# Twice the room for the software DMA queue's descriptors, and two DRAM writes placed later in the loop

## The chip, the cores and the metric

The kernel runs on one core of one Trainium2 chip. The metric is the device time of one execution in microseconds. The kernel before takes 748.84 us (median of 3 runs, 746.74 to 749.02).

A core has a matrix engine (TensorE, PE; its weight loads are shown as PEld), VectorE (DVE), ScalarE (ACT), GpSimd (POOL) and a queue for transfers (SyncE, SP). Each engine works through its own list of instructions in order; semaphores tie the lists together. All times of single instructions are from one profiled execution and count from the start of its span.

## What is computed

One layer of a hybrid encoder on 512 frames of width 1024, in float32. Cut to what matters here:

```python
hn   = rms_norm(x, norm1_g)
proj = hn @ w_in                         # q, k, v of two attentions, and two gates
out_a = chunked_attention(qa, ka, va, ...)        # 8 heads x 64, softmax
out_b = stick_breaking_attention(qb, kb, vb)      # 8 heads x 64
mixed = sigmoid(gate_a) * (out_a @ w_branch_a) + sigmoid(gate_b) * (out_b @ w_branch_b)
x = x + mixed @ w_out
hid = rms_norm(x, norm2_g) @ w_ffn_up    # 1024 -> 2 x 2816
hid = causal_depthwise_conv_width_3(hid) + conv_b
gate, up = hid[:, :2816], hid[:, 2816:]
x = x + (silu(gate) * up) @ w_ffn_down   # 2816 -> 1024
```

The change touches the last four lines: the way from the up-projection to the down-projection.

## The kernel before, in words

**Precision.** A float32 product is made of three matmuls in a reduced format: each operand is split into a high part (a cast, on ACT) and a low part (the operand minus the high part, on DVE), and high x high, high x low and low x high are summed. So every weight block that SP loads (`raw`) is split into `whi` (ACT, L271 or L242) and `wlo` (DVE, L276 or L243) before PE can use it. A split of block j+1 is issued while PE works on block j.

**The up-projection** is a loop over 22 blocks of 128 gate columns and 128 up columns (`up0` to `up21`, L1229). Ten blocks are plain products of 128x512 (L300 to L302). Twelve (`SEVEN`) are done with seven products in place of eight, in 128x256 pieces (L1171); their sums of weights were made earlier, put into DRAM (`parked`) and are loaded again by `fetch_extra` (L230) into `wxh`, `wxl`, `w2h`, `w2l`. After a block's products come bias and convolution (`conv`, L990 to L993), SiLU (L1014) and the product of gate and up (L1089) into one of four places of `ub`.

**Pairs.** After every second block, `pair_sums(i)` turns two places of `ub` into the operands of the down-projection. Three sums and one difference are made on DVE (`sums`, L1044), some into `st`, a buffer of which there is one. The results are then split into high and low parts in two tiles: `ax` (the first combination, 2048 wide) and `ay` (the second, 1536 wide). For pair 0 and for pairs 9 and 10, ACT casts and DVE subtracts (`halves`). For pairs 1 to 8, `by_dma` (L1056) does the subtraction in the transfer: ACT writes the negative of the high part into the low part's place (L1061), a transfer on POOL's queue adds the source to it (L1062, `accum_op=ALU.add`), and ACT casts the high part (L1063). That makes four accumulating transfers a pair: in the program's order on POOL `ay<-ub` (128x256), `ax<-st` (128x256), `ax<-ub` (128x768) and `ay<-st` (128x512). The next pair's first sum writes `st`, so it has to wait until `ay<-st` of this pair has landed.

**Kept in DRAM.** `ay` of pairs 0 to 6 is written to `ayd` by POOL right after the pair (L1095); it is read back by `fetch` (L1126) on the same queue. `ax` of pairs 0 and 1 is written to `axd` by SP (L1097) and read back by SP at L1236, after `up18` and after `up21`.

**Order.** The program is written in one order, and a scheduler then sets each engine's list from it (with priorities in a few places). [...]

The lines that the prediction speaks of: L133 to L148 (loads of weight blocks), L230 (parked sums), L161 and L1269 (split and products of the down-projection), L1044, L1061 to L1063, L1089, L1095, L1097, L1126 and L1191.

Of the kernel before, what the change touches and what calls it, by code (L numbers as in the profile page):

```python
# [8 lines left out]
F32 = mybir.dt.float32  # L9
# [6 lines left out]
P = 128  # L16
# [58 lines left out]
def block_kernel(ctx: ExitStack, tc: tile.TileContext, x, xt, params, g2, rbx, wts, wd0, wd1, out):  # L75
    nc = tc.nc
    V, A, G, PE, SP = nc.vector, nc.scalar, nc.gpsimd, nc.tensor, nc.sync
# [4 lines left out]
    sm = ctx.enter_context(tc.tile_pool(name="sm", bufs=1))  # L82
# [5 lines left out]
    def apool(name):  # L88
        return ap_ctx.enter_context(tc.tile_pool(name=name, bufs=1))
# [2 lines left out]
        apool(n) for n in ("pv", "pst", "pqn", "ppt", "pwk", "po")]  # L92
    pool_c = apool("pc")
    pool_pk = apool("ppk")
    par = sm.tile([P, 280], F32, tag="par", name="par")
    A.dma_start(par[:, 0:8], params[:, 0:8])
    A.preload_act_table_set("exp_and_others")
    WARM = 9
# [190 lines left out]
    def run_chunk(key, body, pieces=4):  # L289

        sp = split_gen(pos[key] + 1, pieces)
        for _ in body(*splits.pop(key)):
            next(sp, None)
            yield
        for _ in sp:
            pass
# [17 lines left out]
    axd = dram.tile([2, P, 2048], F32, tag="axd", name="axd")  # L314
# [668 lines left out]
    pairs = {}  # L983
# [4 lines left out]
    def conv(ps, tile_idx, c):  # L988
        cw = lambda j: par[:, C_CW + 2 * NF * j + tile_idx:C_CW + 2 * NF * j + tile_idx + 1]
        tap = A.activation(c, ps, AF.Identity, scale=cw(2), bias=par[:, C_CB + tile_idx:C_CB + tile_idx + 1])  # L990
        late["tap"] = (tap,)
        V.scalar_tensor_tensor(c[:, 1:], ps[:, 0:S - 1], cw(1), c[:, 1:], op0=ALU.mult, op1=ALU.add)
        V.scalar_tensor_tensor(c[:, 2:], ps[:, 0:S - 2], cw(0), c[:, 2:], op0=ALU.mult, op1=ALU.add)  # L993
# [17 lines left out]
    def gate(j, pg):  # L1011
        g = fp.tile([P, S], F32, tag="cg", name=f"cg{j}", bufs=1)
        conv(pg, j, g)
        A.activation(g, g, AF.Silu)  # L1014
        return g
# [68 lines left out]
    def up_fin(j, pg, pu, g=None):  # L1084
        if g is None:
            g = gate(j, pg)
        u = ub[:, j % 4, :]
        conv(pu, NF + j, u)
        late["fin"] = (V.tensor_tensor(u, g, u, op=ALU.mult),)  # L1089
        if j % 2 == 1 and j // 2 < 9:  # L1090
            steps = pair_sums(j // 2)
            for step in steps:
                step()
            if j // 2 < 7:
                G.dma_start(ayd[j // 2], pairs[j // 2][1].bitcast(F32))  # L1095
            if j // 2 < 2:
                SP.dma_start(axd[j // 2], pairs[j // 2][0].bitcast(F32))  # L1097

    def up_body(j):
        def body(hi, lo):  # L1100
            pg, pu = BANK(f"pg{j}", j - 1), BANK(f"pu{j}", j - 1)
            yield from up_mm(pg, hi, lo, 0, 0, S)
            g = gate(j, pg)
            if j in (2, 3):
                next(late["ts"])
            held = [] if j + 1 in SEVEN else None
            yield from up_mm(pu, hi, lo, P, 0, S, held)

            def end():
                for mm in held or ():  # L1110
                    mm()
                up_fin(j, pg, pu, g)
            if held:
                late["end"] = end
            else:
                end()
            if j in (2, 3):
                next(late["ts"])
        return body

    def fetch(i):

        tag = {0: "wxh", 1: "wxl", 6: "ax"}.get(i, "ts")
        n, bufs = {"wxh": (1600, 1), "wxl": (1600, 1), "ts": (2048, 4), "ax": (2048, 6)}[tag]
        ay = fp.tile([P, n], F32R, tag=tag, name=f"ay{i}", bufs=bufs)[:, 0:1536]
        G.dma_start(ay, ayd[i])  # L1126
        pairs[i] = (pairs[i][0], ay)
# [31 lines left out]
    def up_seven(j):  # L1159
        def body(hi, lo, wh, wl):  # L1160
# [40 lines left out]
            V.tensor_tensor(hu[:, left], b7, hu[:, right], op=ALU.add)  # L1201
            V.tensor_tensor(hu[:, right], hu[:, right], pc[:, 1], op=ALU.add)
            up_fin(j, None, hu, g)
            yield
        return body
# [4 lines left out]
    def up_first(j):  # L1210
        def body(hi, lo):
            pg, pu = BANK(f"pg{j}", 0), BANK(f"pu{j}", 0)
            halves.append((hi, lo, pg, pu))
            yield from up_mm(pg, hi, lo, 0, 0, 256)
            yield from up_mm(pu, hi, lo, P, 0, 256)
            if j == 1:
                n = 0
                for i, (h, l, g, u) in enumerate(halves):
                    for o, ps in ((0, g), (P, u)):
                        for _ in up_mm(ps, h, l, o, 256, S):  # L1220
                            n += 1
                            if n == 1 or 4 <= n < 8:
                                next(late["ts"])
                            yield
                    up_fin(i, g, u)
        return body

    late["ts"] = token_sums()
    for j in range(NF):  # L1229
        body = up_first(j) if j < 2 else up_seven(j) if j in SEVEN else up_body(j)  # L1230
        for _ in run_chunk(f"up{j}", body, pieces=4 if j < 2 else 2):
            pass
        if j in (SECOND[-1] + 1, SEVEN[-1] + 1):
            i = int(j == SEVEN[-1] + 1)
            ax = fp.tile([P, 2048], F32R, tag=("w2l", "ts")[i], name=f"ax{i}b", bufs=(1, 4)[i])
            SP.dma_start(ax.bitcast(F32), axd[i])  # L1236
            pairs[i] = (ax, pairs[i][1])
            for k in range(5 * i):
                fetch(k)
# [196 lines left out]
```

## Time and profile before

| what | value |
|---|---|
| median of 3 runs | 748.84 us (746.74 to 749.02) |
| the profiled execution | 752.24 us |
| its span, first to last instruction | 750.5 us |
| mean granted clock of PE | 0.986 |
| busy: PE, DVE, ACT, POOL | 720.6, 587.7, 432.7, 86.0 us |
| transfers of the software queue | 7264 packets, 20.45 MB |
| transfers of SP's and ACT's queues (hardware) | 133.81 MB |

How to read it: the engines work beside each other, so a busy time is no share of the sum. An engine's idle time is of use only where it is the engine that sets the end, and here PE is busy for 96% of the span. The profile tells for an idle stretch what ended it ("<-"); where a wait is for several things, it is put down to the one that came last by its records. "issue" means that nothing that the profile shows was waited for. The table of stretches gives each engine's busy microseconds between two times.

### The profile page before, as it was taken

The page shows a single profiled execution, that of the slowest core. Times are in us where ns is not written, and L with a number is a line of the kernel's source. Part 1 is how long each engine was busy: PE and PEld are TensorE (multiplying, and loading weights), DVE is VectorE, ACT ScalarE, POOL GpSimd, SP SyncE. Part 2 cuts the span into 40 slices and gives each one's busy share as a digit, 9 for nine tenths or more (in the row PEclk, how much of TensorE's full clock was granted, in tenths as well). Part 3 has the DMA queues.
Part 4 walks back from the last instruction along what each step waited for, and adds up shares of the span by engine and source line. Part 5 has one row for each costly group of instructions (what it writes and reads, how often), then busy time and mean ns, then how long its engine had stood idle before and what let it go on. Part 6 is the DMA issues. An engine that isn't in the chain of part 4 may idle for free.

```text
span 750.5 us, 11266 instructions
## 1 busy us (share of the span) xinstructions
PE 720.6 (96%) x4091; PEld 630.7 (84%) x4091; DVE 587.7 (78%) x1049; ACT 432.7 (58%) x803; POOL 86.0 (11%) x123
## 2 busy tenths in 40 slices
PE   9999999999999999999999998986998979999997
PEld 7889998888988888888898898885988869788886
DVE  6678779778999998694667985475848849899687
ACT  7486567577767675342365675455747745544541
POOL 2501300001111121000030011111111121000000
PEclk9999999999999999999999999998998989999999
DMA  9713336352563655769579589875766859765463
GB/s 320 273 58 97 100 106 216 127 196 113 169 221 143 190 203 206 253 228 339 222 280 295 211 261 310 241 219 160 232 169 183 253 141 339 269 211 196 169 224 112
DMA packets 51863, 154.97 MB, mean 206 GB/s; under 512 B 5600, under 2 KB 12384, under 8 KB 44000
## 3 DMA queue, kind: packets, MB, share of 16 engines
q1 hardware_dynamic: 44256, 133.67, 50.7%
q0 software_dynamic: 7264, 20.45, 10.6%
q8 instruction: 32, 0.52, 0.3%
q14 instruction: 23, 0.19, 0.1%
q10 hardware_dynamic: 288, 0.14, 0.1%
HBM read 116.49 MB, written 30.41 MB: 196 GB/s over the span
## 4 chain that ended last, share of the span: by engine, by line
PE 79%; DMA 6%; issue 6%; ACT 4%; DVE 4%; POOL 0%; DVEq 0%; SPq 0%; ACTq 0%; POOLq 0%
PE P L1269 13%; PE p L1171 8%; DMA ay<-st 4%; PE vA L433 3%; PE uA L433 3%; PE gB L300 2%; PE qkB L302 2%; PE gB L301 2%; PE qkB L300 2%; PE gB L302 2%; PE qkB L301 2%; PE wo L300 2%; PE wo L302 2%; PE wo L301 2%; PE pg L300 2%
## 5 line engine op out<-in xcount | busy, mean ns | idle before, releaser
L165 ACT CAST whi_dn<-raw_dn 128x1024 fp32r<-128x1024 f32 x33 | 34.4, 1050 | 26.2 <-DMA raw_dn<-in_wd 13.5
L1269 PE MATMUL P<-whi_dn,ax 128*128 128x512 f32 x144 | 44.7, 390 | 0.0
L161 DVE TENSOR_TENSOR wlo_dn<-raw_dn,whi_dn 128x1024 fp32r<-128x1024 f32 x33 | 40.1, 1223 | 3.6 <-ACT whi_dn L165 3.6
L300 PE MATMUL pg<-hth,whi_up 128*128 128x512 f32 (+1 forms) x96 | 34.9, 364 | 7.2 <-ACT whi_up L271 7.2
L1269 PE MATMUL P<-whi_dn,ay 128*128 128x512 f32 x132 | 40.8, 389 | 0.0
L744 POOL TENSOR_SCALAR_AFFINE_SELECT bB<-bB 128x128 f32<-128x128 f32 x32 | 21.9, 688 | 143.9 <-DVE bB L743 135.2
L1171 PE MATMUL p<-ts,whi_up 128*128 128x256 f32 x192 | 37.0, 288 | 0.0
L1044 DVE TENSOR_TENSOR st<-ub 128x256 f32<-128x256 f32 x11 | 4.6, 421 | 40.1 <-DMA ay<-st 31.5
L1171 PE MATMUL p<-hth,whi_up 128*128 128x256 f32 x96 | 28.2, 294 | 8.0 <-ACT whi_up L242 8.0
L302 PE MATMUL pg<-hth,wlo_up 128*128 128x512 f32 (+1 forms) x96 | 34.7, 361 | 1.2 <-DVE wlo_up L276 1.2
L301 PE MATMUL pg<-htl,whi_up 128*128 128x512 f32 (+1 forms) x96 | 34.7, 362 | 0.0
L207 DVE TENSOR_TENSOR pkr<-pkr 128x512 f32<-128x512 f32 x40 | 27.4, 685 | 8.7 <-DMA pkr<-in_wts 4.3
L300 PE MATMUL pu<-hth,whi_up 128*128 128x512 f32 (+1 forms) x90 | 31.8, 354 | 0.2 <-DVE hg L1197 0.2
L1269 PEld LDWEIGHTS P<-whi_dn,ax 128*128 128x128 f32 x144 | 27.0, 188 | 5.9 <-ACT whi_dn L165 0.3
L301 PE MATMUL pu<-htl,whi_up 128*128 128x512 f32 (+1 forms) x90 | 31.8, 353 | 0.0
L302 PE MATMUL pu<-hth,wlo_up 128*128 128x512 f32 (+1 forms) x90 | 31.5, 350 | 0.0
L1171 PEld LDWEIGHTS p<-ts,whi_up 128*128 128x128 f32 x192 | 31.2, 199 | 0.1
L1171 PE MATMUL p<-hth,wlo_up 128*128 128x256 f32 x96 | 28.1, 293 | 2.7 <-DVE wlo_up L243 2.7
L1171 PE MATMUL p<-ts,wlo_up 128*128 128x256 f32 x96 | 27.8, 289 | 2.6 <-DVE wlo_up L243 2.6
L243 DVE TENSOR_TENSOR wlo_up<-raw_up,whi_up 128x1024 fp32r<-128x1024 f32 x24 | 28.8, 1217 | 0.6 <-ACT whi_up L242 0.6
L1269 PEld LDWEIGHTS P<-whi_dn,ay 128*128 128x128 f32 x132 | 24.8, 188 | 5.1
L1269 PE MATMUL P<-wlo_dn,ax 128*128 128x512 f32 x72 | 28.1, 391 | 0.9 <-DVE wlo_dn L161 0.9
(350 smaller groups left out, 2566.9 us busy)
## 6 DMA issues: line engine op xcount, KB each, us to landing
parked<-pkr SPq DMA_DIRECT2D x45, 256.0 KB, 3.0
raw_dn<-in_wd SPq DMA_DIRECT2D x11, 1024.0 KB, 5.4
pkr<-in_wts SPq DMA_DIRECT2D x10, 1024.0 KB, 6.9
raw_up<-in_wts SPq DMA_DIRECT2D x10, 1024.0 KB, 6.6
raw_up<-in_wts SPq DMA_DIRECT2D x12, 512.0 KB, 6.1
raw_dn<-in_wd SPq DMA_DIRECT2D x11, 512.0 KB, 3.4
wxl_up<-parked SPq DMA_DIRECT2D x21, 256.0 KB, 5.9
ayd<-ay POOLq DMA_DIRECT2D x7, 768.0 KB, 3.9
```

Source lines behind the costliest of these rows:

```text
L161: chain("halves", V.tensor_tensor(o, x, y, op=op))
L165: chain("casts", A.copy(hi[:, sl], src))
L207: V.tensor_tensor(b[o], b[x], b[y], op=op)
L243: V.tensor_tensor(l[:, sl], src[:, sl], h[:, sl].bitcast(F32), op=ALU.subtract)
L300: ins = PE.matmul(ps, sh, mh, start=first, stop=False)
L301: PE.matmul(ps, sh, ml, start=False, stop=False)
L302: PE.matmul(ps, sl, mh, start=False, stop=last)
L433: PE.matmul(pss[t], st[:, 4 * half + k, t * P:(t + 1) * P], mv[:, k, :], start=half == 0 and k == 0 and j == 0, stop=half == 1 and k == 3 ...
L744: G.affine_select(b[:, n - P:n], b[:, n - P:n], pattern=[[-1, P]], compare_op=ALU.is_gt, fill=0.0, base=0, channel_multiplier=1)
L1044: return [V.tensor_tensor(o, x, y, op=op) for o, x, y, op in ((s1, u0[:, hi_], u1[:, hi_], ALU.add), (u0[:, hi_], u0[:, lo_], u0[:, hi_], ...
L1171: PE.matmul(ps, st, mv[:, k, :], start=first and k == 0 and n == 0, stop=last and k == 3 and n == 2, skip_group_check=True)
L1269: chain("products", PE.matmul(dst, st, mv, start=first and n == 0, stop=last and n == 2, skip_group_check=True))
```

## The change

Three edits. The region for the software queue's descriptors becomes 1024 bytes of a partition instead of 512. The tile `par`, of which 186 columns are used, is cut from 280 to 192 columns, 352 bytes a partition. The writes of `ax` to `axd` are no longer in `up_fin`, after pairs 0 and 1 (blocks 1 and 3); they are in the loop over blocks, after block 6 for pair 0 and after block 9 for pair 1.

```diff
-    par = sm.tile([P, 280], F32, tag="par", name="par")
+    par = sm.tile([P, 192], F32, tag="par", name="par")
...
             if j // 2 < 7:
                 G.dma_start(ayd[j // 2], pairs[j // 2][1].bitcast(F32))
-            if j // 2 < 2:
-                SP.dma_start(axd[j // 2], pairs[j // 2][0].bitcast(F32))
...
         for _ in run_chunk(f"up{j}", body, pieces=4 if j < 2 else 2):
             pass
+        if j in (6, 9):
+            SP.dma_start(axd[j // 9], pairs[j // 9][0].bitcast(F32))
...
-    nc = bacc.Bacc("TRN2", target_bir_lowering=False, num_devices=1, dynamic_dma_scratch_size=512)
+    nc = bacc.Bacc("TRN2", target_bir_lowering=False, num_devices=1, dynamic_dma_scratch_size=1024)
```

What the scheduler makes of it is seen in the engines' lists. First SP, at the second write to `axd` (pair 1), in the kernel before; `raw_up` is the load of a weight block in three parts, `wxl_up`, `w2h_up` and `w2l_up` are parked sums, and the numbers behind the names count the buffers as the program makes them:

```order
L230 DMA wxl_up_4767<-parked 128x512
L141 DMA raw_up_4762<-in_wts 128x512
L142 DMA raw_up_4762<-parked 128x512
L143 DMA raw_up_4762<-in_wts 128x1024
L1097 DMA axd<-ax_4593 128x2048
L230 DMA w2h_up_4904<-parked 128x512
L230 DMA w2l_up_4905<-parked 128x512
```

The same place on SP in the changed kernel:

```order
L230 DMA wxl_up_4765<-parked 128x512
L141 DMA raw_up_4760<-in_wts 128x512
L142 DMA raw_up_4760<-parked 128x512
L143 DMA raw_up_4760<-in_wts 128x1024
L1232 DMA axd<-ax_4592 128x2048
L230 DMA w2h_up_4902<-parked 128x512
L230 DMA w2l_up_4903<-parked 128x512
```

The write comes from another line of the code (L1232 instead of L1097) and stands between the same two loads; the first write to `axd`, 13 rows earlier, has kept its place as well. Only the buffers' numbers differ. POOL's list at pair 1 and the start of pair 2, in the kernel before:

```order
L1062 DMA ay_4594<-ub 128x256
L1062 DMA ax_4593<-st_4595 128x256
L1062 DMA ax_4593<-ub 128x768
L1062 DMA ay_4594<-st_4595 128x512
L1095 DMA ayd<-ay_4594 128x1536
L1062 DMA ay_4851<-ub 128x256
```

And in the changed kernel:

```order
L1062 DMA ay_4593<-ub 128x256
L1062 DMA ax_4592<-st_4594 128x256
L1062 DMA ax_4592<-ub 128x768
L1062 DMA ay_4593<-st_4594 128x512
L1095 DMA ayd<-ay_4593 128x1536
L1062 DMA ay_4849<-ub 128x256
```

Nothing has moved here either. The lists of all five engines are the same in both kernels, row by row, and so are the semaphores that each instruction waits for; addresses of tiles differ, and lines behind L1095 are counted two lower up to L1230 (L1126 is L1124 there).

## The prediction

> **What bounds the kernel now.** I read the busy times by stretch first, then who waited for whom, then the time lines of POOL, DVE and ACT around those waits. In the stretch view a row gives the stretch, its length, the busy us of PE, PEld, DVE, ACT and POOL with counts, the granted clock, the DMA share and GB/s.
>
> ```profile
> 438.00:618.00 180.00, 156.83 (x1044) 143.63 (x1044) 121.10 (x195) 108.24 (x188) 30.14 (x37) 0.95 0.74 213
> ```
>
> This is the up-projection with its pairs. PE is idle for 180.00 - 156.83 = 23.2 us of it, while DVE and ACT are far from full. PE is what the kernel is made of, so any gain must come out of these 23.2 us. Who ended PE's waits in the whole run, with total, count and longest:
>
> ```profile
> PE p L1171 <- ACT whi_up L242: 8.0, 2, 4.7
> PE pg L300 <- ACT whi_up L271: 7.2, 1, 7.2
> PE p L1171 <- DVE wlo_up L243: 5.3, 4, 2.1
> PE pg L302 <- DVE wlo_up L276: 1.2, 1, 1.2
> PE p L1171 <- DMA w2h_up<-parked: 1.2, 1, 1.2
> ...
> PE P L1269 <- DVE wlo_dn L161: 0.9, 1, 0.9
> ```
>
> The first five are the idle time of the stretch (22.9 of 23.2): PE wants the next weight block, and its high part (ACT) or low part (DVE) isn't made. A split is one cast and one subtraction a half, so they came late because something stood ahead of them in their queues:
>
> ```profile
> DVE st L1044 <- DMA ay<-st: 31.5, 5, 8.4
> ACT ax L1061 <- DVE st L1044: 30.7, 5, 8.4
> ```
>
> DVE stands at the first sum of a pair (L1044, into the only st buffer) until the last accumulating transfer of the pair before, the one that reads st, has landed; ACT stands behind DVE at L1061. The gaps also cost clock. More rows of the stretch view, the first three right after the three longest PE gaps, the last three without any gap:
>
> ```profile
> 512.25:519.08 6.83, 4.65 (x11) 3.69 (x12) 5.81 (x8) 6.83 (x11) 0.85 (x1) 0.50 0.51 145
> 566.87:573.70 6.83, 6.19 (x29) 6.19 (x30) 6.39 (x8) 6.83 (x10) 1.73 (x2) 0.50 0.47 119
> 614.65:621.48 6.83, 5.07 (x22) 4.78 (x23) 6.54 (x8) 6.83 (x10) 1.72 (x2) 0.50 0.65 139
> 391.00:459.00 68.00, 68.00 (x456) 62.24 (x455) 51.60 (x74) 40.20 (x63) 4.91 (x7) 1.00 0.77 249
> 520.00:564.00 44.00, 44.00 (x299) 40.70 (x297) 29.12 (x50) 23.56 (x42) 7.01 (x9) 1.00 0.70 197
> 619.00:651.00 32.00, 32.00 (x173) 27.57 (x171) 27.37 (x40) 15.74 (x24) 3.56 (x6) 0.96 0.94 333
> ```
>
> At half clock the matmuls of the first three rows took 4.65 + 6.19 + 5.07 = 15.9 us; at full clock they take 8.0 us less.
>
> Why the last transfer of a pair lands so late stands on POOL (start, duration, what it issues, idle time before it); below it the time to landing of the first three transfers, asked one at a time:
>
> ```profile
> 438.32 0.93 POOL L1062 DMA_DIRECT2D ay<-ub  x1 [4.87 <-ACT ay L1063]
> 444.18 0.86 POOL L1062 DMA_DIRECT2D ax<-st  x1 [4.92 <-ACT cg L1014]
> 448.02 0.87 POOL L1062 DMA_DIRECT2D ax<-ub  x1 [2.98 <-ACT cg L990]
> 452.28 0.85 POOL L1062 DMA_DIRECT2D ay<-st  x1 [3.39 <-issue]
> 459.96 0.56 POOL L1095 DMA_DIRECT2D ayd<-ay  x1 [6.83 <-DMA ay<-st]
> 460.57 0.87 POOL L1062 DMA_DIRECT2D ay<-ub  x1
> ```
>
> ```profile
> DMA to landing us min/median/max: 5.5/5.5/5.5
> DMA to landing us min/median/max: 3.5/3.5/3.5
> DMA to landing us min/median/max: 4.0/4.0/4.0
> ```
>
> 438.32 + 5.5 = 443.8, and the second goes out at 444.18; 444.18 + 3.5 = 447.7, the third at 448.02; 448.02 + 4.0 = 452.0, the fourth at 452.28. Each leaves 0.3 us after the one before it has landed; the releasers named in brackets are ACT instructions that don't make its input. So one accumulating transfer is in flight at a time. A plain one beside it is allowed: at 460.57 an accumulating one follows the plain write of ayd at once. Two accumulating ones don't fit, one and a plain one do. I read this as descriptor room: it is what the change doubles.
>
> **The change part by part.** *The write of axd.* The instructions of all five engines stand in the same places with the same waits before and after; the loop's later statement is scheduled where the old one was. Cost and gain: nothing by itself. What stands there still matters: SP waits at the second write, with six parked loads and a weight load queued behind it.
>
> ```profile
> SPq L1097 <- DMA ax<-ub: 10.3, 1, 10.3
> ```
>
> It waits for the third transfer above (issued 448.02, landed 452.0). That wait shrinks with the room; the 1.2 us in which PE waits for w2h is its price and goes with it.
>
> *The smaller par tile and the addresses.* No instruction more or less; what lies behind it moves by 512 - 352 = 160 bytes. No row shows an effect of an address; I take 0, with either sign inside the measurement's spread.
>
> *The room.* In units of the old room, a plain transfer with an accumulating one fits and two accumulating ones don't, so an accumulating one needs more than a half. Plain ones show its other end: the loads of ay are held only at the fourth.
>
> ```profile
> 628.74 0.54 POOL L1126 DMA_DIRECT2D ay<-ayd  x1 [0.50 <-PE p L1171]
> 634.23 0.53 POOL L1126 DMA_DIRECT2D ay<-ayd  x1 [4.95 <-DMA raw_dn<-in_wd]
> 636.88 0.53 POOL L1126 DMA_DIRECT2D ay<-ayd  x1 [2.12 <-issue]
> ```
>
> The third leaves at 628.74, the fourth only 5 us later, and the fifth stands for 2.1 us with no releaser shown. So a plain one takes over a quarter, and an accumulating one between a half and three quarters. Doubled room holds two of them surely, three if one takes up to two thirds. I take three. When each transfer of the first pair could leave is set by ACT's copies of its negative (L1061), of which these are the first and the last of four:
>
> ```profile
> 437.48 0.41 ACT L1061 ACTIVATE ay<-ub 128x256 fp32r<-128x256 f32 x1
> ...
> 442.38 0.64 ACT L1061 ACTIVATE ay<-st 128x512 fp32r<-128x512 f32 x1
> ```
>
> All four are ready by 442.38 + 0.64 = 443.0, against a fourth issue at 452.28. With three in flight the fourth leaves when the first has landed, 443.8 + 0.3 = 444.1. Its landing is bounded by the 3.5 above and by its own old time, 459.45 - 452.28 = 7.2; I take 7.2, since the transfers now share the engines, so 451.3. DVE asks for st behind this row:
>
> ```profile
> 453.01 0.69 DVE L1089 TENSOR_TENSOR ub<-cg,ub 128x512 f32<-128x512 f32 x1
> 459.45 0.42 DVE L1044 TENSOR_TENSOR st<-ub 128x256 f32<-128x256 f32 x1 [5.75 <-DMA ay<-st]
> ```
>
> That is at 453.7: 2.4 us to spare, and the 5.75 us wait is gone. The longest wait, late in the stretch, began at 610.21 - 8.37 = 601.8 (rows below). The fourth transfer that it waited for was ready long before it left:
>
> ```profile
> 590.49 0.63 ACT L1061 ACTIVATE ay<-st 128x512 fp32r<-128x512 f32 x1
> ```
>
> ```profile
> 599.90 0.85 POOL L1062 DMA_DIRECT2D ax<-ub  x1 [4.29 <-issue]
> 606.23 0.87 POOL L1062 DMA_DIRECT2D ay<-st  x1 [5.47 <-issue]
> ```
>
> ```profile
> 601.42 0.42 DVE L1191 TENSOR_TENSOR hu<-p,pc 128x256 f32<-128x256 f32 x1
> 610.21 0.42 DVE L1044 TENSOR_TENSOR st<-ub 128x256 f32<-128x256 f32 x1 [8.37 <-DMA ay<-st]
> ```
>
> Ready at 591.1, issued at 606.23: 15 us of nothing but the queue. Leaving by 595 it lands by 602.2.
>
> [...] DVE does nothing between 601.84 and 610.21, and POOL still issues only at 606.23; and 0.85 to 0.93 us for an issue is the same whether DVE works or not. [...]
>
> *The sum.* PE's gaps 23.2 us and the half clock 8.0 us make 31.1 that can go. What is late next: DVE is busy 121.1 us, which fits into 180 - 31 = 149 at 81%; ACT at 73%. Not every wait need vanish. A short one that remains costs what this did, after which PE waited the 1.2 us for the wlo of L276 and 0.2 more:
>
> ```profile
> 586.12 0.43 DVE L1044 TENSOR_TENSOR st<-ub 128x256 f32<-128x256 f32 x1 [3.15 <-DMA ay<-st]
> ```
>
> So 1.4 us for a wait of 3.15: from 0 to 7 pairs, 0 to 9.8 us; the gapless rows of 68, 44 and 32 us are nearer to 0. I take 2.0, one or two such waits. Net 31.1 - 2.0 = 29.1 us. The profiled execution took 752.24 (span 750.5), 3.4 above the median of 748.84; 752.24 - 29.1 = 723.1, and from the median 748.84 - 29.1 = 719.7, say 720.
>
> **The rivals.** *Only two fit.* The fourth then leaves when the second has landed. The second is ready between 437.9 and 443.0; from the middle, 440.4 + 7.2 + 0.3 = 447.9, and the fourth lands at 455.1, 1.4 us after DVE asks. Taking PE's 1.4 us at half of seven pairs more, 5 us: 725. For it: the bound of three quarters; against: only the upper quarter of that range gives it. 0.10.
>
> *The room isn't what holds them.* [...] Then only the fourth plain transfers move, no PE wait hangs on them, and the time is 749. Serial by nature has 0.07, the lock-out 0.01.
>
> *Slower: the loads become the bound.* In 149 us instead of 180 the same bytes are 213 x 180 / 149 = 257 GB/s, and the share of 0.74 becomes 0.89. If the weight loads then land so late that each of some 16 blocks (of the loop's 22) loses 2.3 us at the split, 37 - 31 = 6 us are lost: 755. It decides at 31 / 16 = 1.9 us a block. Against it stand the gapless rows with 249 and 333 GB/s at shares of 0.77 and 0.94. [...] The trace has the waits at the issue, so I give this rival 0.04.
>
> **How the numbers follow.** My forecast, three in flight, has 0.78; with the rivals' 0.10, 0.08 and 0.04 that is 1. Low end: all 31.1, the 0.9 at L1269 and the 2.1 by which the fastest run lies under the median: 748.84 - 34.1 = 714.7, 715. High end: 31.1 less 9.8 is 21.3, 727.5; with the 2.1 the other way 729.6, 730, which takes in the case of two. What is left out is 0.12 and the tails. Under 0.3%, 2.2 us, a measurement of this kernel can't tell from no change: the runs lie 2.3 us apart. Faster 0.78 + 0.10 = 0.88, same 0.08, slower 0.04.
>
> **What would show it.** Right: on POOL the second and third accumulating transfer of a pair follow ACT's L1061 by under 1 us; DVE's wait at L1044 falls from 31.5 us to under 8; PE busy in the up stretch is over 97%, and the clock stays at 1.00 in it. Two in flight: the third of a pair leaves 0.3 us after the first lands. Wrong: POOL's issues still 0.3 us behind each landing (the room isn't it), or PE waits for whi_up behind "DMA raw_up" rows (the loads).

## The result and the profile after

The changed kernel takes 724.68 us (median of 4 runs, 724.38 to 724.95) against 748.93 (median of 4, 746.74 to 750.88): a ratio of 0.9677, 95% interval 0.9650 to 0.9704. It is faster by 24.2 us, inside the range forecast; the number forecast, 720.0, was 4.7 us too low. The profiled execution took 724.38 us.

The page of the changed kernel, its span and the busy times of the engines:

```profile
span 722.6 us, 11266 instructions
PE 717.1 (99%) x4091; PEld 624.9 (86%) x4091; DVE 589.2 (82%) x1049; ACT 433.1 (60%) x803; POOL 85.7 (12%) x123
```

PE was busy for 720.6 us of 750.5 before; now it is busy for 717.1 of 722.6. The idle time is gone, while PE's busy time has fallen by only 3.5 us, although 8.0 us of half clock should have gone out of it. That is the first sign that PE's work itself has become a little dearer.

The up-projection with its pairs in the stretch view of the changed kernel, and the stretch behind it (columns as in the prediction):

```profile
438.00:594.00 156.00, 156.00 (x1107) 145.08 (x1106) 127.90 (x203) 113.61 (x195) 30.76 (x38) 1.00 0.89 261
594.00:625.00 31.00, 31.00 (x169) 26.55 (x168) 28.86 (x42) 16.52 (x24) 3.22 (x6) 1.00 0.88 327
```

PE has no gap left and its clock is full. The DMA share is 0.89 and the rate 261 GB/s, as the prediction worked out for this stretch (0.89 and 257), and PE waits for no load. Who ended PE's waits in the whole run of the changed kernel:

```profile
PE warm L352 <- DVE warm L349: 1.1, 1, 1.1
PE gA L300 <- DVE mixA L622: 0.3, 1, 0.3
```

Both lie ahead of the up-projection and stand in the kernel before as well. The waits behind them, on DVE and on SP's queue, in the changed kernel:

```profile
DVE st L1044 <- DMA ay<-st: 2.5, 2, 2.3
```

```profile
SPq L1232 <- DMA ax<-ub: 8.4, 1, 8.4
```

DVE waits 2.5 us instead of 31.5. (In the kernel before a sixth wait of DVE at L1044, 8.6 us up to 486.21, is put down to "issue"; the `ay<-st` before it, issued at 478.81, took 7.3 us to land, so that wait was of the same kind, and the sum of before is 40.1.) SP's wait for `ax` has fallen only from 10.3 to 8.4, but the wait of PE for `w2h_up`, 1.2 us, is gone.

The first pair, in the time lines of POOL and ACT in the changed kernel; below them the time to landing of the first and of the fourth transfer:

```profile
442.45 0.91 POOL L1062 DMA_DIRECT2D ay<-ub  x1 [5.17 <-ACT ay L1063]
443.77 0.85 POOL L1062 DMA_DIRECT2D ax<-st  x1 [0.41 <-ACT ax L1063]
446.05 0.87 POOL L1062 DMA_DIRECT2D ax<-ub  x1 [1.42 <-ACT ax L1061]
447.57 0.85 POOL L1062 DMA_DIRECT2D ay<-st  x1 [0.65 <-ACT ay L1061]
```

```profile
442.94 0.40 ACT L1061 ACTIVATE ax<-st 128x256 fp32r<-128x256 f32 x1
444.78 0.84 ACT L1061 ACTIVATE ax<-ub 128x768 fp32r<-128x768 f32 x1
446.51 0.64 ACT L1061 ACTIVATE ay<-st 128x512 fp32r<-128x512 f32 x1
```

```profile
DMA to landing us min/median/max: 4.2/4.2/4.2
DMA to landing us min/median/max: 7.5/7.5/7.5
```

The second, third and fourth transfers leave 0.42 to 0.43 us after ACT has written their negative (442.94 + 0.40 = 443.34 to 443.77; 445.62 to 446.05; 447.15 to 447.57). The third leaves before the first lands at 442.45 + 4.2 = 446.7 and the second at 449.6, so three are in flight. The fourth lands at 447.57 + 7.5 = 455.1. DVE asks for `st` at 459.27 (458.58 + 0.69) and doesn't wait:

```profile
458.58 0.69 DVE L1089 TENSOR_TENSOR ub<-cg,ub 128x512 f32<-128x512 f32 x1
459.31 0.42 DVE L1044 TENSOR_TENSOR st<-ub 128x256 f32<-128x256 f32 x1
```

The 8.4 us wait of before at 610.21 (pair 8) is the one that is left in part, 2.3 us. There the fourth transfer of the pair ahead leaves at 572.77, 0.42 us after ACT (571.71 + 0.64), so the room no longer holds it; but it takes 11.1 us to land:

```profile
572.77 0.84 POOL L1062 DMA_DIRECT2D ay<-st  x1 [0.43 <-ACT ay L1061]
584.00 0.42 DVE L1044 TENSOR_TENSOR st<-ub 128x256 f32<-128x256 f32 x1 [2.25 <-DMA ay<-st]
```

One thing in this profile was not forecast: the same work ahead of the up-projection has become slower. The out-projection (`wo`), which comes after 1809 matmuls in both kernels, starts at 330.0 us before and at 334.4 after, and PE doesn't wait in between for anything new. The matmuls of `uA`, first in the kernel before and then in the changed one, show where it comes from (duration in ns as minimum, median and maximum; then the first and last start; behind the arrow first the matmul's moving operand, then its stationary one, the one that PEld loads):

```profile
L433 PE MATMUL uA<-whi_uA,hth x28: 389/389/397, 8.9 to 27.3; 128*128 128x512 f32 x28
```

```profile
L433 PE MATMUL uA<-whi_uA,hth x28: 392/396/401, 7.9 to 26.9; 128*128 128x512 f32 x28
```

Each lasts 7 ns longer, and from start to start it is 234 ns in place of 227 (medians).

### The profile page after: what moved, and what is told of

Read it like the earlier page. It is cut to its first block, busy times and chain, and to the rows that moved or that the text cites. A ratio compares the mean times of both kernels' runs of the same rounds, so it can differ in the third digit from the quotient of the medians.

```text
span 722.6 us, 11266 instructions
## 1 busy us (share of the span) xinstructions
PE 717.1 (99%) x4091; PEld 624.9 (86%) x4091; DVE 589.2 (82%) x1049; ACT 433.1 (60%) x803; POOL 85.7 (12%) x123
## 3 DMA queue, kind: packets, MB, share of 16 engines
q0 software_dynamic: 7264, 20.45, 10.8%
## 4 chain that ended last, share of the span: by engine, by line
PE 97%; DVE 1%; DMA 1%; SPq 0%; issue 0%; DVEq 0%
PE p L1169 16%; PE P L1269 15%; PE vA L433 3%; PE uA L433 3%; PE pg L302 3%; PE pg L301 3%; PE pg L300 3%; PE pu L302 2%; PE pu L300 2%; PE pu L301 2%; PE gB L301 2%; PE gB L300 2%; PE qkB L301 2%; PE qkB L302 2%; PE qkB L300 2%; PE gB L302 2%
## 5 line engine op out<-in xcount | busy, mean ns | idle before, releaser
L1269 PE MATMUL P<-whi_dn,ax 128*128 128x512 f32 x144 | 44.8, 391 | 0.0
L161 DVE TENSOR_TENSOR wlo_dn<-raw_dn,whi_dn 128x1024 fp32r<-128x1024 f32 x33 | 40.1, 1223 | 4.8 <-ACT whi_dn L165 4.8
L1269 PE MATMUL P<-whi_dn,ay 128*128 128x512 f32 x132 | 41.0, 391 | 0.0
L1169 PE MATMUL p<-ts,whi_up 128*128 128x256 f32 x192 | 35.1, 278 | 0.0
L1269 PEld LDWEIGHTS P<-whi_dn,ax 128*128 128x128 f32 x144 | 27.1, 188 | 5.8
L1169 PEld LDWEIGHTS p<-ts,whi_up 128*128 128x128 f32 x192 | 29.3, 188 | 0.1
L1269 PEld LDWEIGHTS P<-whi_dn,ay 128*128 128x128 f32 x132 | 24.8, 188 | 5.2
L742 DVE TENSOR_TENSOR_SCAN aB<-aB,reset 128x127 f32<-128x127 f32 (+3 forms) x32 | 25.9, 816 | 3.0 <-ACT aB L737 3.0
L1269 PE MATMUL P<-wlo_dn,ax 128*128 128x512 f32 x72 | 28.1, 391 | 0.0
L1169 PE MATMUL p<-htl,whi_up 128*128 128x256 f32 x96 | 26.9, 280 | 0.0
```

The source lines that it names most:

```text
L161: chain("halves", V.tensor_tensor(o, x, y, op=op))
L742: V.tensor_tensor_scan(ar, ar, reset[:, S - n:S - 1][:, ::-1], 1.0, op0=ALU.mult, op1=ALU.max)
L1169: PE.matmul(ps, st, mv[:, k, :], start=first and k == 0 and n == 0, stop=last and k == 3 and n == 2, skip_group_check=True)
L1269: chain("products", PE.matmul(dst, st, mv, start=first and n == 0, stop=last and n == 2, skip_group_check=True))
```

## The experiments

Theory R: the room alone makes the gain. Rival W: the later writes of `axd` move something. Theory A: the displacement of 160 bytes makes matmuls slower, and takes back what is missing. The expectations use these letters. All edits are against the kernel before unless said, and in each the engines' lists are the same row by row. Tiles behind `par` keep their addresses when the room and `par` together stay at 1632 bytes a partition; "displaced by n bytes" means n more than that.

| run | room, bytes | displaced by | median us | ratio to before (95%) |
|---|---|---|---|---|
| axd_only | 512 | 0 | 749.46 | 1.0015 (0.9987 to 1.0043) |
| shift160_room512 | 512 | 160 | 753.73 | 1.0059 (1.0037 to 1.0082) |
| room576_same_addr | 576 | 0 | 717.84 | 0.9594 (0.9574 to 0.9613) |
| room768_same_addr | 768 | 0 | 717.69 | 0.9584 (0.9548 to 0.9620) |
| room832_same_addr | 832 | 0 | 718.20 | 0.9584 (0.9551 to 0.9617) |
| room768_shift32 | 768 | 32 | 725.21 | 0.9696 (0.9678 to 0.9715) |
| room768_shift64 | 768 | 64 | 724.92 | 0.9692 (0.9674 to 0.9711) |
| room768_shift128 | 768 | 128 | 723.73 | 0.9670 (0.9643 to 0.9697) |
| the changed kernel | 1024 | 160 | 724.68 | 0.9677 (0.9650 to 0.9704) |
| room1024_shift192 | 1024 | 192 | 722.50 | 0.9661 (0.9643 to 0.9679) |
| room768_weights32 | 768 | split weights alone, 32 | 731.17 | 0.9770 (0.9739 to 0.9802) |
| room1024_weights_back | 1024 | 160, split weights 256 or 0 | 723.78 | 0.9672 (0.9645 to 0.9699) |
| room576_back256 | 576 | -256 | 717.87 | 0.9588 (0.9536 to 0.9640) |

### The later writes alone

```diff
-            if j // 2 < 2:
-                SP.dma_start(axd[j // 2], pairs[j // 2][0].bitcast(F32))
...
+        if j in (6, 9):
+            SP.dma_start(axd[j // 9], pairs[j // 9][0].bitcast(F32))
```

> The kernel before with the later statement of the two writes alone; room 512 and par 280 as before. Theory R (the whole gain is descriptor room): ratio to the kernel before 1.000 within 0.3%, 749 us, PE's waits in the profile between 22 and 26 us as before. Rival W (moving the writes frees the loads queued behind them on SP): at least the wait for w2h goes with what follows from it, 2 us or more, 747 us or less.

No difference that can be measured (12 runs): the interval leaves at most 1 us of gain, and rival W needs 2. The stretch of the up-projection in this run, and the waits of PE and of DVE:

```profile
438.00:618.00 180.00, 160.95 (x1057) 147.81 (x1056) 124.36 (x199) 111.46 (x193) 30.46 (x38) 0.93 0.75 217
```

```profile
PE pg L300 <- ACT whi_up L271: 7.0, 1, 7.0
PE p L1169 <- ACT whi_up L242: 4.9, 1, 4.9
...
DVE st L1044 <- DMA ay<-st: 29.5, 5, 8.6
```

The gaps and the half clock are there. PE's gaps in the stretch, 180.00 - 160.95 = 19.1 us, are 4 us shorter than in the profile of before and under the 22 to 26 expected; its clock is lower (0.93 instead of 0.95). Single runs of the kernel before differ by as much (744.5 to 753.0 us). PE's wait for `w2h` is still there too, 1.5 us. Rival W falls.

### The displacement alone

```diff
-    par = sm.tile([P, 280], F32, tag="par", name="par")
+    par = sm.tile([P, 320], F32, tag="par", name="par")
```

> The kernel before with par at 320 columns instead of 280: room as before, and every tile behind par 160 bytes further on, the same addresses as in the changed kernel. The two large tiles hth and htl stay where they are. Theory A (the 160 bytes slow the matmuls that read hth or htl together with a tile that moved): the gA matmuls take 393 to 398 ns in the median instead of 389, wo stays at 389, the start of wo comes 4 us later than in the kernel before, and the time is slower by 4 to 7 us, 753 to 756, ratio 1.005 to 1.009. Rival V (the longer matmuls of the changed kernel's profile are of that execution, or come with its denser transfers): no change of the matmuls, 749 us, ratio 1.000.

Slower by 0.59%, 0.37 to 0.82%, or 4.4 us, with nothing changed but addresses. Its `uA`:

```profile
L433 PE MATMUL uA<-whi_uA,hth x28: 392/397/400, 8.8 to 27.7; 128*128 128x512 f32 x28
```

These are the durations of the changed kernel, to 1 ns. The medians of the three groups of `gA` are 392, 394 and 398, where 393 to 398 was expected. Its `wo` starts at 335.2 us, 5.2 after the 330.0 of before, and is at 389 as before. Theory A holds. Here the room is old and PE still waits in the up-projection, so the slower matmuls there can use up waiting time; 4.4 us is therefore a lower price than that of a PE without gaps.

### The room alone, in three sizes

The edit for 832 bytes; for 768 and 576 the numbers are 216 and 264 columns.

```diff
-    par = sm.tile([P, 280], F32, tag="par", name="par")
+    par = sm.tile([P, 200], F32, tag="par", name="par")
...
-    nc = bacc.Bacc("TRN2", target_bir_lowering=False, num_devices=1, dynamic_dma_scratch_size=512)
+    nc = bacc.Bacc("TRN2", target_bir_lowering=False, num_devices=1, dynamic_dma_scratch_size=832)
```

> Room 832 and par 200 columns, 320 bytes more and 320 bytes less, so that every tile behind par keeps the address of the kernel before; the writes of axd as before. [...] Theory A (addresses): no PE waits and the matmuls of gA back at 389 ns, so 724.7 less 4 to 6 us: 719 to 721, ratio 0.960 to 0.963. Rival V: as the changed kernel, 724 to 725, ratio 0.968. If the room doesn't do for three, the third transfer of a pair leaves 0.3 us after the first has landed, and up to 5 us come on top.

> Room 768 (half as much again) and par 216 columns, so that the addresses are those of the kernel before; the writes of axd as before. Two accumulating transfers fit, three don't (three would need more than three halves of the old room). The prediction's rival of two in flight: the third of a pair leaves 0.3 us after the first has landed, DVE still waits 1 to 3 us for st at some pairs, PE loses about 5 us more than with three: 724 to 726. If two are enough to hide the transfers, PE has no waits in the up-projection and the time is that of room 832, 719 to 721 under theory A.

> Room 576, par 264 columns, addresses of the kernel before. [...] PE's waits under 3 us, 718 to 722 us. If an accumulating one takes more than 18 of 32 parts, one at a time stays, DVE's wait at L1044 stays near 40 us and the time near 748.

All three take 718, about 30 us less than before and 7 less than the changed kernel; theory A's 719 to 721 was a little high, since it priced the displacement at 4 to 6 us. The stretch view of the run with 768, and its waits of PE (all of them) and of DVE for `st`:

```profile
438.00:590.00 152.00, 152.00 (x1078) 142.35 (x1077) 126.82 (x200) 112.59 (x195) 30.90 (x38) 1.00 0.90 263
```

```profile
PE warm L352 <- DVE warm L349: 1.1, 1, 1.1
PE gA L300 <- DVE mixA L622: 0.3, 1, 0.3
```

```profile
DVE st L1044 <- DMA ay<-st: 2.8, 2, 2.1
```

The two waits of DVE, 2.1 and 0.7 us, cost PE nothing. How many transfers fit differs between the sizes, and the time doesn't. POOL's first pair with 768 bytes, then with 576:

```profile
438.34 0.93 POOL L1062 DMA_DIRECT2D ay<-ub  x1 [4.87 <-ACT ay L1063]
439.66 0.86 POOL L1062 DMA_DIRECT2D ax<-st  x1 [0.38 <-ACT ax L1063]
443.07 0.85 POOL L1062 DMA_DIRECT2D ax<-ub  x1 [2.55 <-ACT ay L1061]
445.24 0.86 POOL L1062 DMA_DIRECT2D ay<-st  x1 [1.32 <-ACT hg L1194]
```

```profile
438.45 0.91 POOL L1062 DMA_DIRECT2D ay<-ub  x1 [4.84 <-ACT ay L1063]
440.70 0.88 POOL L1062 DMA_DIRECT2D ax<-st  x1 [1.35 <-ACT ub L990]
443.99 0.86 POOL L1062 DMA_DIRECT2D ax<-ub  x1 [2.41 <-ACT ay L1063]
446.62 0.86 POOL L1062 DMA_DIRECT2D ay<-st  x1 [1.77 <-issue]
454.98 0.86 POOL L1062 DMA_DIRECT2D ay<-ub  x1 [2.10 <-ACT ay L1063]
```

With 768 the second leaves at once, and the third at 443.07, 0.3 us after the first has landed (442.76): two in flight. With 576 there are two as well, but the write of `ayd` ahead of the pair, which lands at 440.40, doesn't fit beside them: the second leaves 0.3 us after that. With 832 three fit, but not with a plain write beside them: later in that run a third leaves at 541.63, 0.3 us after the write of `ayd` has landed (541.32), though ACT had its input ready at 538.8:

```profile
537.04 0.56 POOL L1095 DMA_DIRECT2D ayd<-ay  x1 [6.99 <-ACT hg L1194]
537.67 0.87 POOL L1062 DMA_DIRECT2D ay<-ub  x1
538.28 1.15 POOL L1062 DMA_DIRECT2D ax<-st  x1
541.63 0.85 POOL L1062 DMA_DIRECT2D ax<-ub  x1 [2.20 <-ACT ay L1063]
```

If what each transfer takes simply adds up, an accumulating transfer takes over 256 bytes of a partition (two don't fit in 512) and at most 277 (three fit in 832); a plain one takes over 128 (with 512, the fourth load is held) and at most 170 (three loads fit). These are estimates from the issues and landings of these runs; what a transfer keeps in the region no row shows. They agree with the two waits for the write of `ayd`: three accumulating transfers leave under 64 of 832 bytes, and two leave under 64 of 576, less than a plain one takes. The 18 of 32 parts in the expectation for 576 are of the old 512 bytes: 288, half of 576; the bound of 277 lies under that.

### Which displacement costs

Three runs as with 768 bytes, with `par` of 224, 232 and 248 columns (32, 64 and 128 bytes more), and the changed kernel with `par` of 200 columns in place of 192:

```diff
-    par = sm.tile([P, 192], F32, tag="par", name="par")
+    par = sm.tile([P, 200], F32, tag="par", name="par")
```

> Room 768 with par at 224 columns: 32 bytes further on than in the kernel before, otherwise as room 768 at the same addresses (717.7 us). Theory A32: gA at 392 to 398 ns, 723 to 726 us. Rival A128: also slower, as anything but a whole number of 128 is. Together with the shifts of 64 and 192 it tells the step.

> Room 768 with par at 232 columns: 64 bytes further on. Theory A32: gA at 389 ns, 717 to 719 us. Rival A128: slower by 4 to 7 us, 722 to 725.

> The changed kernel with par at 200 columns instead of 192: tiles behind par stand 192 bytes further on than in the kernel before, instead of 160. Theory A32 (a matmul is slowed when its two SBUF operands have moved against each other by an odd multiple of 32 bytes): gA back at 389 ns, wo at its old start, 717 to 719 us, ratio 0.957 to 0.960. Rival A128 (it takes a whole number of 128 or more bytes to restore them): as the changed kernel, 724 to 726, ratio 0.968.

> Room 768 with par at 248 columns: tiles behind par 128 bytes further on than in the kernel before. Shifts of 32, 64, 160 and 192 bytes were all slower by 4 to 8 us. If the step is 128 bytes: gA, qkB and gB back at 389 ns, 717 to 719 us. If it is 256 or more: 722 to 726 us.

Every displacement tried, 32, 64, 128, 160 and 192 bytes, costs 0.8 to 1.2% against the ratio of 0.9584. The one of 192 is the cheapest, 1.5 us under the range of rival A128; the table at the end of the next section shows why. So it isn't that tiles have to stand a multiple of 32, 64 or 128 bytes from their old places. The forms of theory A by which one of these would be free, A32 among them, fall.

### What it is displaced against

In the changed kernel `wo` is as fast as before, though its operands have moved by 160 bytes too:

```profile
L300 PE MATMUL wo<-whi_wo,mh x64: 389/389/478, 330.0 to 377.3; 128*128 128x512 f32 x64
```

```profile
L300 PE MATMUL wo<-whi_wo,mh x64: 388/390/480, 334.4 to 381.7; 128*128 128x512 f32 x64
```

The slow products are those that read `hth` or `htl` and, in the down-projection, those that read `ax` and `ay` of the last two pairs. These four lie in pools that are laid out from the other end of the partition (`side="right"`) and so don't move with `par`; the split weights do. In `wo` both operands move together. That suggests the distance between a matmul's two operands. Two runs test it. The first leaves all as with 768 bytes and moves only the split weights, by 8 columns (32 bytes) inside their tiles (those of the down-projection too, which the expectation leaves out by mistake):

```diff
-        wh, wl = (late["pool"].tile([P, w], F32R, tag=tag, name=f"{tag}_up{j}")[:, 16:1552] for tag, w in tags)
+        wh, wl = (late["pool"].tile([P, w], F32R, tag=tag, name=f"{tag}_up{j}")[:, 24:1560] for tag, w in tags)
...
-        sh = 48 if key[:2] in ("qA", "kA", "vB") else 16 if key in ("up0", "up1") or is_seven(i) else 0
+        sh = 56 if key[:2] in ("qA", "kA", "vB") else 24 if key in ("up0", "up1") or is_seven(i) else 8
```

> Room 768, par 216, every tile at the address of the kernel before; only the place of the split weights inside their own tiles is moved by 8 columns, 32 bytes, in all blocks up to up21 (split weights of the down-projection excepted). If it is the distance between the split weights and hth or htl that counts: the matmuls of uA to gB and of the up blocks slower by 3 to 8 ns each, wo at 389, 722 to 726 us. If it is another tile's place (what ACT and DVE read and write at the time): 717 to 719 us.

The second is the changed kernel with the split weights moved back, so that they stand 256 or 0 bytes from their old place:

```diff
-        wh, wl = (late["pool"].tile([P, w], F32R, tag=tag, name=f"{tag}_up{j}")[:, 16:1552] for tag, w in tags)
+        wh, wl = (late["pool"].tile([P, w], F32R, tag=tag, name=f"{tag}_up{j}")[:, 40:1576] for tag, w in tags)
...
-        sh = 48 if key[:2] in ("qA", "kA", "vB") else 16 if key in ("up0", "up1") or is_seven(i) else 0
+        sh = 8 if key[:2] in ("qA", "kA", "vB") else 40 if key in ("up0", "up1") or is_seven(i) else 24
```

> The changed kernel with the split weights moved inside their tiles by 96 bytes on or 160 back, so that they stand a whole number of 256 bytes from where they stood in the kernel before; other tiles stay 160 bytes further on. If the distance of the split weights to hth and htl is what counts, with a step of 256 or less: uA to gB at 389 ns, 717 to 719 us, ratio 0.958 to 0.960. If not: 724 to 725 us.

The first takes 731.17, 13.5 us more than with the weights in place and over the 722 to 726 expected. Nothing but weights moved, and now `wo` is slow too (392/396/477 ns) and the down-projection as well (medians of 394 to 396 ns); I had expected `wo` at 389 and the down-projection as before, which was wrong, since their weights moved against `mh` and against `ax` and `ay`. The second run, in the matmuls of `uA` and of `wo`:

```profile
L433 PE MATMUL uA<-whi_uA,hth x28: 389/389/398, 8.3 to 26.7; 128*128 128x512 f32 x28
```

```profile
L300 PE MATMUL wo<-whi_wo,mh x64: 392/394/476, 331.0 to 379.6; 128*128 128x512 f32 x64
```

In `uA` the distance of the operands is 256 bytes more than before, and the 389 of before is back. In `wo` the weights have moved by 256 and `mh` by 160, and it is slow. By 331.0, where `wo` starts, most of the loss ahead of it is gone. But the total is only 0.9 us below the changed kernel, because `wo`, `yB` and the down-projection lost what the others gained; the 717 to 719 us that theory A gave for this run was missed for that reason.

If 256 bytes count as nothing, then a displacement of all tiles behind `par` by 256 is free, though `hth` stays. That can be had with less room:

```diff
-    par = sm.tile([P, 280], F32, tag="par", name="par")
+    par = sm.tile([P, 200], F32, tag="par", name="par")
...
-    nc = bacc.Bacc("TRN2", target_bir_lowering=False, num_devices=1, dynamic_dma_scratch_size=512)
+    nc = bacc.Bacc("TRN2", target_bir_lowering=False, num_devices=1, dynamic_dma_scratch_size=576)
```

> The kernel before with a room of 576 bytes and par of 200 columns: room and par together take 256 bytes less than before, so every tile behind them stands 256 bytes from its old place, while hth, htl and the tiles laid out from the other end stay. If only the distance of a matmul's two operands modulo 256 bytes counts, nothing is lost: uA lasts 389 ns in the median, gA (L300) 387 to 389, wo starts at 329 to 331 us, and the time is 717 to 719 us, as with 576 bytes and the old addresses. If any displacement against hth costs, as 32, 64, 128, 160 and 192 bytes did, uA lasts 393 to 397 ns, wo starts near 334, and the time is 722.5 to 725.

717.87 us, the same as with 576 bytes and the old addresses (717.84). Its `gA`, whose weights have moved by 256 bytes against `hth`, and then that of the run with the displacement alone, by 160:

```profile
L300 PE MATMUL gA<-hth,whi_gA x64: 387/389/501, 85.3 to 182.1; 128*128 128x512 f32 x64
```

```profile
L300 PE MATMUL gA<-hth,whi_gA x64: 388/392/503, 87.4 to 185.8; 128*128 128x512 f32 x64
```

So what counts is the distance of the two operands, and 256 bytes more or less count as nothing. With the addresses from the built programs, every 128x512 matmul of the twelve runs, of before and of after that another one follows can be put down by the distance of its moving operand from the stationary operand of the matmul behind it (the start-to-start times are those of the traces, up to 300 ns). In all but 127 of them its own stationary operand stands at the same distance, so the table can't tell which of the two counts:

| distance modulo 256 | matmuls | mean ns from start to start |
|---|---|---|
| 0 | 17177 | 227.9 |
| 64 | 1133 | 229.7 |
| 32 | 1067 | 233.4 |
| 96 | 2335 | 233.7 |
| 128 | 1133 | 232.6 |
| 160 | 688 | 234.2 |
| 192 | 1132 | 233.4 |
| 224 | 1923 | 233.3 |

In the kernel before all of them stand at 0. In the changed kernel 881 stand at 96 and 252 at 160, with means of 233.8 and 234.3 ns; 770 are left at 0. In the run with a displacement of 192 the 881 stand at 64, the cheapest place but 0, with a mean of 229.8.

The means of the table are over different matmuls. The same ones compared say the same: against the run with 768 bytes, in the ten other runs with more room, a 128x512 product that stays at 0 differs by 0.1 ns on average, and one moved from 0 to 96 is 5.8 ns longer. A 128x256 product that stays at 192 is 0.3 ns shorter, and one moved from 192 to 0 is 3.3 ns longer.

## Why the prediction was right, and where it was off

**What bounds the kernel: right.** The gain came out of PE's gaps and the half clock of the up-projection, and both are now zero there.

**The write of axd, taken at nothing: right.** Alone it gave a ratio of 1.0015.

**The room as the cause, three in flight: right, and shown.** With 1024 bytes three accumulating transfers are in flight, and in the first pair each leaves when ACT is done, not 0.3 us behind a landing. Where transfers are ready faster, one plain and three accumulating ones go out at once, and a fourth accumulating one waits until the plain one and the first have landed (550.46):

```profile
544.29 0.56 POOL L1095 DMA_DIRECT2D ayd<-ay  x1 [6.38 <-ACT hg L1192]
544.92 0.85 POOL L1062 DMA_DIRECT2D ay<-ub  x1
545.53 1.12 POOL L1062 DMA_DIRECT2D ax<-st  x1
546.46 1.09 POOL L1062 DMA_DIRECT2D ax<-ub  x1
550.76 0.85 POOL L1062 DMA_DIRECT2D ay<-st  x1 [3.22 <-ACT whi_up L242]
```

The landing taken at 7.2 us was 7.5; DVE had 4.2 us to spare where 2.4 was worked out. For the longest wait the prediction took the same 7.2 us ("Leaving by 595 it lands by 602.2"), which is 0.4 us after DVE asks by its own rows; there the landing took 11.1 us, and 2.3 of 8.4 us of DVE's wait stayed.

**The leftover waits, 2.0 us: too much.** The runs with the addresses kept show what the room is worth by itself: 748.17 - 717.69 = 30.5 us with 768 bytes, between the 29.1 of the forecast and the 31.1 that could go. PE's waits in the stretch of the pairs are 0 in all three (with 576 bytes 0.3 us is left at 429.4, ahead of the first accumulating transfer). The price of 1.4 us of PE for a DVE wait of 3.15 doesn't scale down: waits of 2.1 and 0.7 us cost nothing.

**The addresses, taken at 0: the step that failed.** The prediction's step was "No row shows an effect of an address; I take 0, with either sign inside the measurement's spread". They cost about 7 us: 724.68 in the changed kernel against 717.69 at the old addresses, or 1% of the time by the ratios 0.9677 and 0.9584. Of the 6.8 us between the two profiled spans (722.6 and 715.8), 4.9 are there when `wo` starts (334.4 and 329.5). The matmuls' own times account for it: compared one by one with the run with 768 bytes, from start to start, the 881 take 4.8 us more, the 252 take 1.6, and all the others together 0.6. With the room at 30.5 and this at -7.0 the sum is 23.5; 24.2 was measured. That no row of the kernel before shows it is true: a trace with one set of addresses can't. But then nothing in it bounded that cost at the spread of the measurement either: each ns on 4091 matmuls is 4.1 us. The code held a hint: `par` reserved 94 columns that nothing used, and the split weights start 0, 16 or 48 columns into tiles that are 64 columns wider than they need; with these places every 128x512 product of the kernel before stands at a distance of 0. That the time still fell into the range is owed to its width of 15 us, not to this step.

**The rival of two in flight: its mechanism was mispriced.** With 768 and 576 bytes two are in flight, and the time is 718, not 725. It put the fourth transfer's landing 1.4 us after DVE asks; with 768 it lands at 450.27 and DVE takes `st` at 453.7. The landing took 5.0 us, with two in flight, in place of the 7.2 that the kernel before shows with one and the 7.5 of the changed kernel with three; no run shows why. That the measured time of the changed kernel lies near the 725 of this rival is chance: it had three in flight.

**The other rivals fell.** The room is what holds the transfers: a change of the room alone, with `par` cut by as much, gives the whole gain. No run shows what the 0.08 was given to, transfers that are serial by nature or a lock-out of POOL: two accumulating transfers were in flight with 576 and 768 bytes and three with 832 and 1024, and an issue took 0.87 us with DVE idle (at 606.23 in the kernel before) and 0.87 with DVE busy throughout (at 446.05 in the changed kernel). The loads didn't become the bound at a share of 0.89 to 0.90. The gain was 30 us, because the time that a transfer stood at its issue was what DVE, and then PE, waited for.

**What stays open.** From the profiled execution of before to the one with 768 bytes the span falls by 750.5 - 715.8 = 34.7 us; the gaps (23.2), the half clock (8.0) and the wait at L1269 (0.9) make 32.1. The other 2.6 us lie at the edges of PE's waits, which the prediction didn't count: compared one by one, 22 matmuls next to these waits and outside the half clock took 3.1 us longer in the kernel before, from start to start with the idle time taken off. Small differences of the rest cancel to within 0.5 us. Why the operands' distance matters isn't shown. A room of 1024 bytes with a displacement of 256 wasn't tried: room and `par` together would take 1888 bytes a partition, 64 more than the most that a run here had (1824).

## What to carry to other kernels

Where a queue's transfers each leave a fixed short time behind a landing (0.3 us here), and the releaser named isn't what makes their input, look for room that they share, and raise it only as far as needed: here 64 bytes a partition more gave the time that 256 and 320 more gave (717.8 against 717.7 and 718.2). A change of a reserved size or of a small tile moves everything behind it, so test it with the addresses kept as well: here the moved addresses took back 7 of 30 us, and the best versions measured are those with 576 to 832 bytes at the old addresses or 256 bytes from them, 717.7 to 718.2 us. Compare the time of single instructions of the costliest groups before and after; a few ns on each of thousands of matmuls show in no wait.

## What the runs showed of the hardware that was not expected

- The time of a matmul depends on where its moving and its stationary operand stand to each other in a partition, and a displacement of 256 bytes changed nothing (717.87 us against 717.84): counted modulo 256, 128x512 products take 227.9 ns from start to start at a distance of 0, 229.7 at 64 and 232.6 to 234.2 at the others. The width matters too: the 128x256 products are fastest at 192 (mean 115.8 ns of 13,289, counted up to 180 ns) and slower at 0 (120.1 of 1,478). Where the nanoseconds are lost these rows don't show.
- An accumulating transfer of the software queue (POOL's: its issues add up to the 20.45 MB of that queue) takes more room than a plain one, by the bounds above 1.5 to 2.2 times as much (over 256 to 277 bytes of a partition, against over 128 to 170). Its width didn't change this: 256, 512 and 768 columns are held alike (issues at 444.18, 452.28 and 448.02 in the kernel before, each 0.3 us behind a landing).
- POOL shows no wait of its own when the room is full: it stands idle until 0.3 us after a landing, and the profile names "issue" or some older instruction as the releaser (in the kernel before a landing at 452.0, the next issue at 452.28, put down to "issue"; a landing at 447.7, the next issue at 448.02, put down to ACT's L990).
